# Gate and up products of 18 of 22 inner chunks as seven quarter products, in a float32 decoder trunk

## The chip, the core and the metric

The kernel runs on one core of a Trainium2 chip. The metric is the device time of one execution in microseconds (us). Engines: PE is TensorE, DVE VectorE, ACT ScalarE, POOL GpSimd, SP SyncE; each runs its own instructions in their order and waits on semaphores of the others. SP's and POOL's queues start transfers here.

## What is computed

A decoder trunk of two layers on 512 tokens of width 1024, all in float32. Six sub-layers, each with a norm before it and one behind it:

```python
def rms_norm(x, g):  return x * rsqrt(mean(x * x, -1) + 1e-6) * g
def swiglu(n, w_gate, w_up, w_down):          # 1024 -> 2816 -> 1024
    return (silu(n @ w_gate) * (n @ w_up)) @ w_down
...
f = swiglu(rms_norm(h, ffn_pre_g[layer, 0]), ...)
h = h + 0.5 * rms_norm(f, ffn_post_g[layer, 0])
h = h + rms_norm(mixer(rms_norm(h, mix_pre_g[layer])), mix_post_g[layer])
f = swiglu(rms_norm(h, ffn_pre_g[layer, 1]), ...)
h = h + 0.5 * rms_norm(f, ffn_post_g[layer, 1])
```

The mixer is a gated spatial unit (gMLP) in layer 0 and multi-head latent attention (MLA) in layer 1; between the layers keys and values are compressed once (`Shared`). The order is FFN 1, gMLP, FFN 2, Shared, FFN 3, MLA, FFN 4.

## The kernel before

Features lie on partitions, tokens along the free axis; the residual stream h is 8 chunks of 128 features by 512 tokens. TensorE multiplies float32r, so each operand is split exactly into a high and a low part, and each product is three matmuls: high by high, high by low, low by high (`mm3`, L391). The weight is the stationary operand (128x128), the activation the moving one (128 x 256 or 512).

Weights come in units of 512 KB (1024 inputs by 128 outputs, 128x1024 in memory), fetched by SP (`fetch`, L363) into one of WR = 3 raw buffers. `parts` (L369) splits a unit: a cast on ScalarE (tile `wh`), then a subtract on VectorE (`wl`), into one of WS = 6 split buffers. Activations live in SLOTS = 59 buffers of 128x512 (tiles `a`). PSUM banks are `mm`.

Nothing orders the program but a planner at build time, `Flow` (L111). The products are a list of items (L210), run in turn; what other engines do behind them are tasks, generators that yield what they wait for. With every instruction the planner books an estimated duration (`cost`, L77; recorded at L100, which is why nearly every row of the profile says L100) and issues tasks' steps and weight splits where the estimate says that their engine is free. The order on each engine is then fixed.

`ffn` (L651) has 22 inner chunks of 128. Chunks 0 and 1, and then 2, are done for the first half of the tokens (A, 256) and then for the second (B), since the halves of h come one after the other; from chunk 3 on all 512 tokens go at once. A chunk is 2 weights x 8 input chunks x 3 = 48 matmuls. The input is h times the gain, without R, the reciprocal root mean square along tokens: R is found later (`Norm.finish`, L482: squares are summed on POOL, a matmul takes the mean, POOL the root, a matmul `mm<-ident,r` spreads it, ScalarE copies it) and multiplied into the gate product in `glu` (L654), which then does Silu, the product with up, and the split of the result. The up product is not multiplied by R; the norm behind the sub-layer takes that into account (argument `norm` of `project`, L599).

The chunks come in groups (`FGROUPS`); behind each group `project` multiplies the group's chunks by w_down into 8 output chunks, which `Boundary` adds up and, behind the last group, norms and adds to h (L518, L551). `hook` puts the rotary tables into FFN 1, and `Shared` ran behind the first group of FFN 3.

Of the kernel before, what the change touches and what calls it, by code (L numbers as in the profile page):

```python
# [16 lines left out]
P = 128  # L17
# [16 lines left out]
FGROUPS = ((0, 8), (8, 15), (15, 22))  # L34
# [54 lines left out]

class Engine:  # L90
    """An engine, whose instructions are also put into the flow's estimate of time."""
# [19 lines left out]
class Flow:  # L111
    """The order of the program. Work that waits for other engines is a generator, which yields what it
    waits for: a condition (a callable), tensors (a list) or an engine that has less than so much to
    do (a pair). What engines do is followed by an estimate of each instruction's time."""
# [28 lines left out]
    def place(self, key, t, us):  # L143
        """Takes the first time from t on in which the engine has nothing to do."""
# [50 lines left out]
    def reach(self, t):  # L195
        """TensorE's next instruction can start at t: do what is due before."""
# [13 lines left out]
    def drive(self, items, fetch, parts):  # L210
        """Run the items. Units are fetched, and split into parts, before their time where there is room."""
# [14 lines left out]
    def get(self):  # L226
        if self.queue and len(self.raw) < WR:
            j, x = self.queue.pop(0)
            raw = self.fetch(*x)
            n = int(np.prod(x[1]))  # L230
# [3 lines left out]
            self.write(raw, self.dma + 2.0)  # L234
# [25 lines left out]
class Parts:  # L260
    """The two parts of each chunk of a tensor, and which halves of the tokens have been written."""
# [13 lines left out]
def decoder_kernel(ctx: ExitStack, tc: tile.TileContext, a: dict, out: bass.AP):  # L275
# [14 lines left out]
    # names given, units split  # L290
# [29 lines left out]
    # tables and clocks of the engines that the first products wait for  # L320
# [42 lines left out]
    def fetch(src, shape, spare=False):  # L363
        n = shape[0] * shape[1]
# [3 lines left out]

    def parts(raw, src, shape, spare=False):  # L369
        """The parts of each of a unit's chunks; `spare` units take room of activations."""  # L370
# [3 lines left out]
        count[1] += 1  # L374
        res = []
        for c0 in range(0, n, step):
# [10 lines left out]
            res += [(hi[:, x : x + m], lo[:, x : x + m]) for x in range(0, step, m)]  # L387
        return res

# [1 line left out]
    def mm3(ps, w, x, start, stop):  # L391
        """ps += w^T x from the parts of w (stationary) and x (moving)."""
# [30 lines left out]
    def rsqrt(x, n, out=None):  # L423
        """1 / sqrt of a few columns."""
# [14 lines left out]
    def token_mean(acc, lo, hi_, n):  # L439
        """Means of acc's columns over n features, by token on partitions."""  # L440
# [5 lines left out]
    def spread(c, n, diag):  # L446
        """Per-token scalars (token on partition, one column a tile) along the free axis, on all partitions."""
# [8 lines left out]
    class Squares:  # L456
        """Sums of chunks' squares."""
# [14 lines left out]
    class Norm:  # L472
        """Scalars of a pre-norm: R along tokens on all partitions, r by token, e = eps / r^2."""
# [32 lines left out]
    def gained(c, gains, outs, lo, hi_):  # L506
        """Split h[c] times each gain."""
# [10 lines left out]
    class Boundary:  # L518
        """Post-norm of a sub-layer's output, the residual sum, and what the next sub-layers read."""
# [31 lines left out]
        def finish(self, lo, hi_, norm):  # L551
            """For some tokens, whose f is f r where there is a norm before it."""
# [32 lines left out]
        def store(self, bc, lo, hi_):  # L585
            """The kernel's result; f has the gains already."""
# [12 lines left out]
    def project(source, ks, bnd, first, last, norm=None, width=NK):  # L599
        """source(d): the unit of output chunk d; ks(): its input."""  # L600
# [38 lines left out]
    def columns(us, x, rng, kouter):  # L639
        """Products of several column units with some tokens."""  # L640
# [10 lines left out]
    def ffn(i, prev, bnd, hook=None, shared=None):  # L651
        hid = {}

        def glu(f, rng, pg, pu):  # L654
            lo, hi_ = rng
            g = slot()[:, : hi_ - lo]
            norm = prev.norm
            yield norm.known(lo, hi_)
            V.tensor_tensor(g, pg, norm.R[:, lo:hi_], op=ALU.mult)
# [4 lines left out]
            SC.copy(hi[:, lo:hi_], g)  # L664
            V.tensor_tensor(lw[:, lo:hi_], g, hi[:, lo:hi_].bitcast(F32), op=ALU.subtract)
            hs.mark(c, lo, hi_)

# [3 lines left out]
        def run(us, fs, rng, kouter=False):  # L671
            banks = columns(us, prev.outs[0], rng, kouter)
            for j, f in enumerate(fs):
                flow.later(glu(f, rng, banks[2 * j], banks[2 * j + 1]))

        def add(gi, f0, f1):
# [12 lines left out]

            start = f0  # L690
            if gi == 0:
                start = f0 + 3
                kept = {}

                def keep(us, fs, rng, kouter):
                    kept[fs] = us
                    go(us, fs, rng, kouter)

# [7 lines left out]
                item(lambda us: keep(early["u"], q, A, False), (), 0)  # L706
                item(lambda us: go(kept[p], p, B, i > 0), (), 4)
                item(lambda us: go(kept[q], q, B), (), 0)
            for f in range(start, f1):
                item(lambda us, f=f: go(us, (f,), ALL), load(f))  # L710
            if gi == 0 and hook is not None:
                item(lambda us: hook())
            if gi == 0 and shared is not None:
                item(shared.run, shared.loads)
# [3 lines left out]
                lambda: prev.norm, f1 - f0,  # L718
# [154 lines left out]
    def rope_tables():  # L873
# [9 lines left out]
        def parts(x):  # L883
            """x as float32 parts of 12 bits, 12 bits and the rest."""
# [13 lines left out]
        # r less the nearest multiples of 2 pi 2^22, 2 pi 2^11 and 2 pi: exact but for what t collects,  # L898
        # which may take r a little out of range again
# [412 lines left out]
```

## Time and profile before

| | |
|---|---|
| time, median of 3 runs | 2021.34 us (2021.0 to 2021.54) |
| profiled execution, span from first to last instruction | 2020.5 us |
| instructions | 25023 |
| TensorE busy | 1976.6 us, 10064 matmuls |
| VectorE busy | 951.7 us, 1437 instructions |
| ScalarE busy | 717.7 us, 1176 instructions |
| GpSimd busy | 218.3 us, 358 instructions |
| mean granted TensorE clock | 0.993 |

Rows of groups give line, engine, operation, output<-inputs (numbers of tiles left out), shapes and count, then busy us and mean ns of one, and the idle time ahead. Rows of the timeline begin with start and duration in us. Rows of windows begin with the stretch and its length, then busy us of each engine (with instructions), and at the end granted clock, DMA share and GB/s. Rows of the DMA part end with KB each and the median us from issue to landing.

### The profile page before, as it was taken

The page shows a single profiled execution, that of the slowest core. Times are in us where ns is not written, and L with a number is a line of the kernel's source. Part 1 is how long each engine was busy: PE and PEld are TensorE (multiplying, and loading weights), DVE is VectorE, ACT ScalarE, POOL GpSimd, SP SyncE. Part 2 cuts the span into 40 slices and gives each one's busy share as a digit, 9 for nine tenths or more (in the row PEclk, how much of TensorE's full clock was granted, in tenths as well). Part 3 has the DMA queues.
Part 4 walks back from the last instruction along what each step waited for, and adds up shares of the span by engine and source line. Part 5 has one row for each costly group of instructions (what it writes and reads, how often), then busy time and mean ns, then how long its engine had stood idle before and what let it go on. Part 6 is the DMA issues. An engine that isn't in the chain of part 4 may idle for free.

```text
span 2020.5 us, 25023 instructions
## 1 busy us (share of the span) xinstructions
PE 1976.6 (98%) x10064; PEld 1685.8 (83%) x10064; DVE 951.7 (47%) x1437; ACT 717.7 (36%) x1176; POOL 218.3 (11%) x358
## 2 busy tenths in 40 slices
PE   8999999999999999999999999999999999999997
PEld 8888888888888888888888888888878898888886
DVE  6443344635635642333465443343767554234434
ACT  5232223433333432222243332223566553222222
POOL 4000000510001400000041010000521150000001
PEclk9999999999999999999999999999999999999999
DMA  6233333142333133333322233333121213332321
GB/s 205 84 99 94 99 96 113 53 136 73 96 103 108 40 115 94 93 96 104 104 74 84 76 114 97 99 93 97 43 73 63 81 46 105 94 100 88 105 84 43
DMA packets 56149, 184.94 MB, mean 92 GB/s; under 512 B 6176, under 2 KB 10400, under 8 KB 56032
## 3 DMA queue, kind: packets, MB, share of 16 engines
q1 hardware_dynamic: 54016, 179.85, 29.0%
q0 software_dynamic: 720, 2.36, 0.4%
q8 instruction: 79, 1.29, 0.3%
q10 hardware_dynamic: 1296, 1.12, 0.2%
q14 instruction: 38, 0.31, 0.0%
HBM read 181.21 MB, written 2.10 MB: 91 GB/s over the span
## 4 chain that ended last, share of the span: by engine, by line
PE 89%; DVE 5%; POOL 3%; ACT 2%; issue 1%; DMA 0%; SPq 0%; DVEq 0%; POOLq 0%; ACTq 0%
PE mm L100 89%; DVE a L100 3%; ACT a L100 1%; DVE h L100 1%; POOL nt L100 1%; POOL y L100 1%; DVE wl L100 1%; POOL a L100 1%; ACT wh L100 0%; POOL a L931 0%; DMA h<-in_xT 0%; DMA wr<-in_mla_w_o 0%; DVE m L100 0%; DVE x L100 0%; POOL r L100 0%
## 5 line engine op out<-in xcount | busy, mean ns | idle before, releaser
L100 PE MATMUL mm<-a,wh 128*128 128x512 f32 (+1 forms) x5584 | 1568.7, 367 | 3.4 <-ACT wh L100 1.3
L100 PEld LDWEIGHTS mm<-a,wh 128*128 128x128 f32 x5584 | 1009.8, 189 | 171.6 <-DVE a L100 1.8
L100 PE MATMUL mm<-a,wl 128*128 128x512 f32 (+1 forms) x2792 | 1020.7, 366 | 1.5 <-DVE wl L100 1.5
L100 ACT CAST wh<-wr 128x1024 fp32r<-128x1024 f32 (+2 forms) x340 | 344.5, 1017 | 999.3 <-PE mm L100 713.2
L100 PEld LDWEIGHTS mm<-a,wl 128*128 128x128 f32 x2792 | 528.5, 189 | 86.0 <-DVE wl L100 2.0
L100 DVE TENSOR_TENSOR a<-mm,a 128x512 f32<-128x512 f32 (+3 forms) x380 | 228.6, 609 | 709.7 <-PE mm L100 698.9
L100 DVE TENSOR_TENSOR wl<-wr,wh 128x1024 fp32r<-128x1024 f32 (+2 forms) x340 | 403.4, 1190 | 216.4 <-ACT wh L100 204.2
L100 POOL TENSOR_TENSOR a<-a,a 128x256 f32<-128x256 f32 x162 | 139.6, 869 | 1165.7 <-ACT a L100 1162.3
L100 PE MATMUL mm<-a,a 128*128 128x256 f32 (+3 forms) x896 | 131.6, 299 | 2.3 <-ACT a L100 2.3
L100 ACT ACTIVATE a<-a 128x256 f32<-128x256 f32 (+1 forms) x216 | 105.5, 504 | 69.4 <-DVE a L100 68.9
L100 PEld LDWEIGHTS mm<-a,a 128*128 128x128 f32 x896 | 119.8, 191 | 7.5 <-ACT a L100 3.2
L100 DVE TENSOR_TENSOR a<-a,a 128x512 fp32r<-128x512 f32 (+4 forms) x171 | 107.9, 633 | 28.1 <-ACT a L100 21.2
L100 ACT CAST a<-a 128x512 fp32r<-128x512 f32 (+2 forms) x134 | 77.8, 583 | 75.6 <-DVE a L100 74.7
L100 PE MATMUL mm<-wh,a 128*128 128x512 f32 x288 | 93.0, 398 | 0.0
L100 POOL TENSOR_TENSOR y<-x,minus_half 128x2 f32<-128x2 f32 (+1 forms) x28 | 22.1, 788 | 527.7 <-DVE x L100 527.6
L100 ACT ACTIVATE a<-h,vec 128x256 fp32r<-128x256 f32 (+1 forms) x104 | 52.1, 520 | 52.6 <-DVE h L100 50.1
L100 PEld LDWEIGHTS mm<-wh,a 128*128 128x128 f32 x288 | 55.1, 191 | 11.7 <-issue 0.2
L100 DVE SCALAR_TENSOR_TENSOR a<-h,vec,a 128x256 fp32r<-128x256 f32 (+1 forms) x104 | 58.1, 578 | 6.0 <-ACT a L100 5.9
L100 PE MATMUL mm<-wl,a 128*128 128x512 f32 x144 | 56.8, 395 | 0.0
L100 DVE SCALAR_TENSOR_TENSOR h<-a,vec,h 128x256 f32<-128x256 f32 x80 | 48.2, 623 | 0.0
L100 ACT COPY a<-mm 128x512 f32<-128x512 f32 (+1 forms) x66 | 33.3, 512 | 32.7 <-PE mm L100 32.7
L100 DVE TENSOR_TENSOR a<-a,mm 128x256 f32<-128x256 f32 x94 | 36.2, 412 | 15.7 <-PE mm L100 13.4
(83 smaller groups left out, 453.0 us busy)
## 6 DMA issues: line engine op xcount, KB each, us to landing
wr<-in_ffn_w_up SPq DMA_DIRECT2D x88, 512.0 KB, 3.5
wr<-in_ffn_w_gate SPq DMA_DIRECT2D x87, 512.0 KB, 3.6
wr<-in_ffn_w_down SPq DMA_DIRECT2D x64, 448.0 KB, 3.3
wr<-in_ffn_w_down SPq DMA_DIRECT2D x32, 512.0 KB, 3.5
wr<-in_w_in_u SPq DMA_DIRECT2D x16, 512.0 KB, 3.7
wr<-in_w_in_v SPq DMA_DIRECT2D x16, 512.0 KB, 3.6
wr<-in_gmlp_w_out SPq DMA_DIRECT2D x16, 512.0 KB, 3.5
wr<-in_mla_w_o SPq DMA_DIRECT2D x8, 512.0 KB, 3.5
```

The lines of the kernel that those rows point to most:

```text
L100: res = fn(*args, **kwargs)
```

## The change

Chunks 0 to 3 of each FFN stay as they were (`PLAIN = 4`), but for one multiply: the up product is now multiplied by R too. Chunks 4 to 21 form 9 pairs. A pair's product is a 2x2 block product for each of gate and up: the outputs' two chunks by the inputs' two halves (a11, a12, a21, a22 hold 4 input chunks of gate and of up each, 512 KB), times the input's two halves by the tokens' two halves (b11 to b22). Seven products of quarter size replace the eight, in Winograd's form of Strassen's scheme, each with sums of weights or of inputs:

| product | weights | input | accumulates in bank |
|---|---|---|---|
| a11 | a11 (raw buffer x) | b11 | X |
| s2 | x = x + s1 | t2 = b22 - b12 + b11, up to the order of the sums | Y |
| s1 | s1 = a21 + a22 | e1 = b11 - b12 | V |
| a12 | a12 (raw buffer y) | b21 | X, on top |
| s3 | a11 + a21 | n3 = b12 - b22 | Y, on top |
| a22 | a22 | t4 = t2 - b21 | Z |
| s4 | y = y + x | b22 | V, on top |

Each is 2 x 4 x 3 = 24 matmuls of N = 256. Signs are arranged so that only sums of weights occur. s1 and the weights of s3 are made by a load through SP and an accumulating DMA through POOL into the same buffer; x = x + s1 and y = y + x by VectorE.

The seven forms of the input need h times gain times R. `prepare` makes them for each FFN once R of both halves is known: for each of 4 chunks 2 multiplies of 512 columns, 4 sums of 256 and 7 splits of 256. A product is put into the order only once all are there in the planner's book. Behind products, tasks combine the banks (`of_a11` to `of_s4`): p1 copied from X by ScalarE, u2 = p1 - Y, u3 = Y - p1, x = u3 - V (after which V may be accumulated into again), and so on; `out` applies Silu and the product and splits.

Further: groups are 0-8, 8-16, 16-22; WR = 5, WS = 5, SLOTS = 61; the planner's cost of a matmul has another formula; Shared stands behind the last pair of FFN 3, ahead of the last output products; the hook of FFN 1 stands ahead of the pairs.

```diff
-FGROUPS = ((0, 8), (8, 15), (15, 22))
+FGROUPS = ((0, 8), (8, 16), (16, 22))
+PLAIN = 4
+NP = (NF - PLAIN) // 2
+H = S // 2
-WR, WS, SLOTS = 3, 6, 59
+WR, WS, SLOTS = 5, 5, 61
...
-        return max(n * (1 if aps[1].dtype in (F32R, BF16) else 4) / 2370.0, 0.03)
+        return max((n + 31) * (1 if aps[1].dtype in (F32R, BF16) else 4) / 2400.0, 0.03)
...
+            def summed(base, more):
+                t = load_raw(src[base], NK * P)
+                nc.gpsimd.dma_start(t, src[more], accum_op=ALU.add)
+                return t
...
+        def before(self):
+            raw = self.pair.raw
+            if self.name == "s2":
+                V.tensor_tensor(raw["x"], raw["x"], raw["s1"], op=ALU.add)
+
+        def behind(self):
+            raw = self.pair.raw
+            if self.name == "a12":
+                V.tensor_tensor(raw["y"], raw["y"], raw["x"], op=ALU.add)
...
-            V.tensor_tensor(g, pu, g, op=ALU.mult)
+            V.tensor_tensor(u, pu, R, op=ALU.mult)
+            V.tensor_tensor(g, u, g, op=ALU.mult)
...
+        def part(name, src):
+            t = slot(F32R)
+            SC.copy(t[:, :H], src)
+            V.tensor_tensor(t[:, H:], src, t[:, :H].bitcast(F32), op=ALU.subtract)
+            forms.setdefault(name, []).append((t[:, :H], t[:, H:]))
+
+        def prepare():
+            norm = prev.norm
+            yield norm.known(0, S)
+            name, base = prev.gains[0]
+            half = NK // 2
+            for c in range(half):
+                n1, n2, e, t = slot(), slot(), slot(), slot()
+                for n, k in ((n1, c), (n2, c + half)):
+                    V.scalar_tensor_tensor(
+                        n, h[k], col(name, base + k), norm.R, op0=ALU.mult, op1=ALU.mult
+                    )
+                b11, b12, b21, b22 = n1[:, :H], n1[:, H:], n2[:, :H], n2[:, H:]
+                part("b11", b11)
+                V.tensor_tensor(e[:, :H], b11, b12, op=ALU.subtract)
+                V.tensor_tensor(t[:, :H], b22, e[:, :H], op=ALU.add)
+                yield ("V", T_LEAD)
+                part("t2", t[:, :H])
+                part("e1", e[:, :H])
+                part("b21", b21)
+                yield ("V", T_LEAD)
+                V.tensor_tensor(e[:, H:], b12, b22, op=ALU.subtract)
+                part("n3", e[:, H:])
+                V.tensor_tensor(t[:, H:], t[:, :H], b21, op=ALU.subtract)
+                part("t4", t[:, H:])
+                part("b22", b22)
+                yield ("V", T_LEAD)
...
+            ORDER = (("a11", "X", "b11"), ("s2", "Y", "t2"), ("s1", "V", "e1"), ("a12", "X", "b21"),
+                     ("s3", "Y", "n3"), ("a22", "Z", "t4"), ("s4", "V", "b22"))
...
+                for w in range(2):
+                    o = ps[:, w * H : (w + 1) * H]
+                    for k in range(half):
+                        hi, lw = us[0][w * half + k]
+                        th, tl = forms[x][k]
+                        flow.reach(max(flow.when(y) for y in (hi, lw, th, tl)))
+                        at = first and w == k == 0
+                        PE.matmul(o, hi, th, start=at, stop=False, skip_group_check=True)
+                        PE.matmul(o, hi, tl, start=False, stop=False, skip_group_check=True)
+                        end = k == half - 1
+                        PE.matmul(o, lw, th, start=False, stop=end, skip_group_check=True)
...
+            def of_s3(self):
+                u3 = self.t["u3"] = slot()
+                x = slot()
+                yield [self.banks["Y"]]
+                V.tensor_tensor(u3, self.banks["Y"], self.t["p1"], op=ALU.subtract)
+                V.tensor_tensor(x, u3, self.banks["V"], op=ALU.subtract)
+                self.read.add("V")
+                self.out(x, self.f + 1, H)
```

What stands on the engines, first on TensorE in the second FFN, behind chunks 0 to 2 (before: chunk 3 begins; `a` is the input's high and low part):

```order
L100 MATMUL mm_5745<-a_5077,wh_5569 128x512 [waits DVE_49]
L100 MATMUL mm_5745<-a_5078,wh_5569 128x512
L100 MATMUL mm_5745<-a_5077,wl_5570 128x512
L100 MATMUL mm_5745<-a_5079,wh_5569 128x512
L100 MATMUL mm_5745<-a_5080,wh_5569 128x512
```

After the change the same chunk 3 ends with the first row here (bank mm_6889), and then the first pair's products stand in pieces of 3: mm_7039 is a11's bank, mm_7071 s2's, mm_7106 s1's, and a_7014 is the fourth b11. Left out behind the fourth row are pieces of the same kind, 27 matmuls of N = 256 in all ahead of the last two rows.

```order
L104 MATMUL mm_6889<-a_6193,wl_6812 128x512
L104 MATMUL mm_7039<-a_6723,wh_6882 128x256 [waits DVE_49,Activation_49]
L104 MATMUL mm_7039<-a_6723,wh_6882 128x256
L104 MATMUL mm_7039<-a_6723,wl_6883 128x256
...
L104 MATMUL mm_7106<-a_6969,wh_7065 128x256 [waits DVE_49]
L104 MATMUL mm_7106<-a_6969,wl_7066 128x256
L104 MATMUL mm_7039<-a_7014,wh_6882 128x256 [waits Activation_49]
L104 MATMUL mm_7039<-a_7014,wh_6882 128x256 [waits DVE_49]
```

So chunk 4's 48 wide matmuls have given way to pieces that wait for the forms as they come. On VectorE at the same place, before, the products of chunk 3 (bank mm_5745, mm_5746) are combined with one weight split (`wl`) between each two steps:

```order
L100 TENSOR_TENSOR a_5806<-mm_5745,a_5093 128x512 [waits PE_49,Pool_49]
L100 TENSOR_TENSOR wl_5808<-wr_5676,wh_5807 128x1024 [waits DMAHW2_49,Activation_49]
L100 TENSOR_TENSOR a_5806<-mm_5746,a_5806 128x512 [waits PE_49,Activation_49]
L100 TENSOR_TENSOR wl_5812<-wr_5730,wh_5811 128x1024 [waits DMAHW3_49,Activation_49]
L100 TENSOR_TENSOR a_5237<-a_5806,a_5236 128x512 [waits Activation_49,Pool_49]
```

After (a_6195 is R, mm_6888 and mm_6889 chunk 3's products, wr_6357 the buffer x, a_7014 the fourth b11):

```order
L104 TENSOR_TENSOR a_6995<-mm_6888,a_6195 128x512
L104 TENSOR_TENSOR a_6996<-mm_6889,a_6195 128x512 [waits PE_49]
L104 TENSOR_TENSOR wr_6357<-wr_6357,wr_6161 128x1024 [waits DVE_49]
L104 TENSOR_TENSOR a_6995<-a_6996,a_6995 128x512 [waits DVE_49,Activation_49]
L104 TENSOR_TENSOR wl_7130<-wr_6815,wh_7129 128x1024 [waits DMASW4_49]
L104 TENSOR_TENSOR a_6331<-a_6995,a_6330 128x512 [waits Activation_49]
L104 SCALAR_TENSOR_TENSOR a_7008<-h,vec,a_6195 128x512
L104 SCALAR_TENSOR_TENSOR a_7009<-h,vec,a_6195 128x512
L104 TENSOR_TENSOR a_7014<-a_7008,a_7014 128x256 [waits Activation_49]
```

The fourth chunk of the forms is begun behind chunk 3's evacuation and behind weight splits and sums of the first pair. Last, VectorE between two pairs in the second FFN, where before stood the rows of the kind shown above. mm_7858 is the bank Y of the pair that ends, mm_7892 its V, a_7851 its p1; wr_7744 and wr_7777 are the next pair's x and s1:

```order
L104 TENSOR_TENSOR wr_7744<-wr_7744,wr_7777 128x1024 [waits DMASW1_49,DVE_49]
L104 TENSOR_TENSOR wl_7951<-wr_7744,wh_7950 128x1024 [waits PE_49,Activation_49]
L104 TENSOR_TENSOR a_7948<-a_7948 128x256 [waits Activation_49]
L104 TENSOR_TENSOR wl_7986<-wr_7777,wh_7985 128x1024 [waits PE_49,Activation_49]
L104 TENSOR_TENSOR a_7811<-a_7948,a_7810 128x256 [waits Activation_49]
L104 TENSOR_TENSOR a_7983<-mm_7858,a_7851 128x512
L104 TENSOR_TENSOR a_7984<-a_7983,mm_7892 128x512 [waits DVE_49]
```

The last two rows are u3 and x = u3 - V; the next pair's sum x + s1, which waits for an accumulating DMA, and the splits of s2 and s1 now stand ahead of them.

More of the change, by code (lines that the diff above doesn't have):

```diff
@@ L374, in parts @@
         count[1] += 1
+        form = src if isinstance(src, Form) else None
+        if form:
+            form.before()
         res = []
@@ L387, in parts @@
             res += [(hi[:, x : x + m], lo[:, x : x + m]) for x in range(0, step, m)]
+        if form:
+            form.behind()
         return res
@@ L662, in glu, with keep_hidden @@
+            V.tensor_tensor(g, u, g, op=ALU.mult)
+            keep_hidden(f, lo, hi_, g)
+        def keep_hidden(f, lo, hi_, x):
             hs, c = hid[f]
             hi, lw = hs.pairs[c]
-            SC.copy(hi[:, lo:hi_], g)
-            V.tensor_tensor(lw[:, lo:hi_], g, hi[:, lo:hi_].bitcast(F32), op=ALU.subtract)
+            SC.copy(hi[:, lo:hi_], x)
+            V.tensor_tensor(lw[:, lo:hi_], x, hi[:, lo:hi_].bitcast(F32), op=ALU.subtract)
             hs.mark(c, lo, hi_)
+        forms = {}
@@ L688, in go, with product @@
                 run(us, fs, rng, kouter)
+            def product(us, pair, step):
+                begin()
+                pair.product(us, *step)
             start = f0
             if gi == 0:
-                start = f0 + 3
+                start = PLAIN
                 kept = {}
@@ L697, in keep @@
                     go(us, fs, rng, kouter)
+                    flow.later(prepare())
                 p, q = (f0, f0 + 1), (f0 + 2,)
@@ L705, in add @@
                     item(lambda us: early.update(u=us), load(q[0], True), 0)
-                item(lambda us: keep(early["u"], q, A, False), (), 0)
+                item(lambda us: go(early["u"], q, A, False), (), 0)
                 item(lambda us: go(kept[p], p, B, i > 0), (), 4)
-                item(lambda us: go(kept[q], q, B), (), 0)
-            for f in range(start, f1):
-                item(lambda us, f=f: go(us, (f,), ALL), load(f))
+                item(lambda us: go(early["u"], q, B), (), 0)
+                for f in range(f0 + 3, PLAIN):
+                    item(lambda us, f=f: go(us, (f,), ALL), load(f))
             if gi == 0 and hook is not None:
                 item(lambda us: hook())
-            if gi == 0 and shared is not None:
-                item(shared.run, shared.loads)
+            for f in range(start, f1, 2):
+                pair = Pair(f)
+                for step in Pair.ORDER:
+                    item(
+                        lambda us, pair=pair, step=step: product(us, pair, step),
+                        [(Form(pair, step[0]), (NK, P), False)],
+                    )
+            if gi == len(FGROUPS) - 1:
+                item(lambda us: forms.clear())
+                if shared is not None:
+                    item(shared.run, shared.loads)
             project(
@@ L717, in add @@
                 lambda: group["x"], bnd, gi == 0, gi == len(FGROUPS) - 1,
[L718 removed]
+                lambda: None, f1 - f0,
             )
```

98 lines of the change are left out of this document (92 added, 6 removed).

## The prediction

> **What bounds the kernel now.** I read the page first: the busy line, then the chain that ended last.
>
> ```profile
> span 2020.5 us, 25023 instructions
> PE 1976.6 (98%) x10064; PEld 1685.8 (83%) x10064; DVE 951.7 (47%) x1437; ACT 717.7 (36%) x1176; POOL 218.3 (11%) x358
> PE 89%; DVE 5%; POOL 3%; ACT 2%; issue 1%; DMA 0%; SPq 0%; DVEq 0%; POOLq 0%; ACTq 0%
> ```
>
> TensorE is busy 98% of the span, so only fewer or shorter matmuls can save much; VectorE, at 47%, has room on the average, but not at every place. The windows view with TensorE alone, over the second FFN (its 512-token chunks and output products) and over a stretch behind a wait, and the timeline at the end of two FFNs' two-half parts, give the price of a matmul:
>
> ```profile
> 714.00:1020.00 306.00, 306.00 (x1352) 1.00 0.33 100
> 386.20:392.80 6.60, 4.79 (x13) 0.50 0.29 79
> ...
> 388.01 1.23 PE L100 MATMUL mm<-half,y 128*128 128x128 f32 x4 [3.95 <-POOL y L100]
> ...
> 1081.11 5.92 PE L100 MATMUL mm<-a,a 128*128 128x256 f32 x48
> 1086.87 0.63 PE L100 MATMUL mm<-a,wh 128*128 128x512 f32 x2
> ```
>
> 306 us for 1352 matmuls of N=512 is 226.3 ns each, without idle time. 48 matmuls of N=256 start at 1081.11 and the next one at 1086.87: 5.76 us, 120 ns each. Half the width costs 53% of the time. And after an idle time of 3.95 us the granted clock is 0.50 for some 6.6 us.
>
> **The products: gain.** In each FFN 18 chunks of 48 N=512 matmuls (864 x 226.3 ns = 195.5 us) become 9 pairs of 7 x 24 N=256 matmuls (1512 x 120 ns = 181.4 us): 14.1 us less. The seven-for-eight saving of 12.5% shrinks to 7%. Over four FFNs: **-56**. A pair of chunks goes from 21.7 to 20.16 us.
>
> The Trainium skill ("TensorE: Matmul & The Clock Gate", Back-to-back issue gap) gives the warm spacing of isolated matmuls as N/2.4 + 2.5 ns, so 109.2 and 215.8 ns, and says itself that this is too little at small N. By it the gain would be 864 x 215.8 - 1512 x 109.2 = 21.3 us an FFN, 85 in all; the 48-matmul rows say otherwise (120 ns).
>
> **The forms: the largest loss.** The pairs read normed input in seven forms, which can be begun only when the scalars R of both token halves are there, and every product needs all four chunks of its form. R of the second half is copied late in the two-half part; the N=512 stream begins 9 to 14 us behind it:
>
> ```profile
> 35.25 0.37 ACT L100 COPY a<-mm 128x256 f32<-128x256 f32 x1
> 49.01 0.63 PE L100 MATMUL mm<-a,wh 128*128 128x512 f32 x2
> 704.46 0.37 ACT L100 COPY a<-mm 128x256 f32<-128x256 f32 x1 [4.43 <-PE mm L100]
> 713.61 0.63 PE L100 MATMUL mm<-a,wh 128*128 128x512 f32 x2
> 1077.72 0.37 ACT L100 COPY a<-mm 128x256 f32<-128x256 f32 x1 [4.43 <-PE mm L100]
> 1667.35 0.37 ACT L100 COPY a<-mm 128x256 f32<-128x256 f32 x1 [4.63 <-PE mm L100]
> 1677.58 0.63 PE L100 MATMUL mm<-a,wh 128*128 128x512 f32 x2
> ```
>
> Behind that stream's start TensorE has chunk 3 (48 x 226.3 ns = 10.9 us) and then, by the order, 27 matmuls on the first three chunks of the forms (3.2 us; 51 in the first FFN, 6.1 us) before the first one that reads the fourth. So it runs dry at 66.0, 727.7, 1101.0 and 1691.7 us. VectorE's side, from rows that follow each other without a gap:
>
> ```profile
> 20.77 0.68 DVE L100 TENSOR_TENSOR a<-wr,a 128x512 fp32r<-128x512 f32 x1
> 21.38 0.47 DVE L100 SCALAR_TENSOR_TENSOR a<-h,vec,a 128x256 fp32r<-128x256 f32 x1
> ...
> 708.22 2.36 DVE L100 TENSOR_TENSOR wl<-wr,wh 128x1024 fp32r<-128x1024 f32 x2
> 710.49 0.75 DVE L100 TENSOR_TENSOR a<-mm,a 128x256 f32<-128x256 f32 x2
> 711.16 1.22 DVE L100 TENSOR_TENSOR wl<-wr,wh 128x1024 fp32r<-128x1024 f32 x1
> 712.29 0.76 DVE L100 TENSOR_TENSOR a<-a,a 128x256 fp32r<-128x256 f32 x2
> 712.96 0.42 DVE L100 TENSOR_TENSOR a<-mm,a 128x256 f32<-128x256 f32 x1
> ...
> L100 DVE SCALAR_TENSOR_TENSOR a<-h,vec,a 128x512 fp32r<-128x512 f32 x8 | 5.5, 744 | 0.0
> ```
>
> From start to start a 1024-wide split takes 1.14 us, a 512-wide step 0.61, a 256-wide one 0.335; a 512-wide scalar-tensor step 0.744 by its group, less the 0.08 by which such rows overlap, 0.66. By the order VectorE has, from the first normed chunk to the subtract that ends the fourth b11: 8 x 0.66 + 46 x 0.335 + 8 x 1.14 + 4 x 0.61 = 32.2 us; the 8 of 1024 are the pairs' own weight splits and sums, which stand between the forms. It starts at R's copy plus 0.37: ready at 737.0, 1110.3 and 1699.9 us. In the first FFN the fourth b11 is there after 25.2 us of such rows, but between it and the subtract that ends the fourth t2, the next that TensorE needs, lie 15.8 us more by the same steps, mostly the rotary tables' 512-wide rows: 35.6 + 41 = 76.6. The stalls are 10.6, 9.3, 9.3 and 8.2 us: **+37**. At the end of each stands one uncovered cast on ScalarE, a subtract and two handovers (0.37 + 0.42 and some 0.1 each): **+4**. The bounds: VectorE may also stand and wait for a bank in between (+2 each), or part of the 512-wide rows falls ahead of R's second half for another reason (-2 each).
>
> Such stalls are broken up only by pieces of 3 matmuls, so the clock row above applies: of the 6.6 us at clock 0.50 above, 4.79 were busy, 2.4 us lost; four times is 10. If the bits of work between keep the clock, nothing is lost. I take **+8**, 0 to 14.
>
> The Trainium skill ("TensorE: Matmul & The Clock Gate", HAM oscillation) says that TensorE's idle gaps must stay under some 3.4 us, or it falls to half clock; this speaks against a change that opens gaps of 8 to 10 us. The trace agrees: 3.95 us was enough.
>
> **Weights.** A pair moves seven units of 512 KB, not four, two of them by accumulating DMA. Rows of the DMA part and of the groups:
>
> ```profile
> q1 hardware_dynamic: 54016, 179.85, 29.0%
> wr<-in_ffn_w_up SPq DMA_DIRECT2D x88, 512.0 KB, 3.5
> a<-in_w_sT POOLq DMA_DIRECT2D x4, 256.0 KB, 5.3
> L732 POOL DMA_DIRECT2D a<-in_w_sT x4 | 2.3, 568 | 0.0
> ```
>
> 29% of 2020.5 us for 179.85 MB is 1.7 us for 512 KB: seven are 12 of a pair's 20 us, or 15 if an add costs two. The capacity is there. No row shows an accumulating DMA; plain rows bound its landing: 3.5 us if like SP's 512 KB, 10.6 if like two of POOL's 256 KB, one behind the other. I take POOL's 5.3 and half of 1.7 for the other 256 KB: 6.2. What it may take: by the order the buffer for the next pair's x comes free with y = y + x, right behind V's read of the pair before, some 1.2 us into a pair; x and the sum's base load follow (3.5 + 1.7 = 5.2 us): 6.4. On VectorE x = x + s1 and the split of s2 stand ahead of s1's split, which can begin at s3's end and a cast of 1.05 (120 matmuls, 14.4 us, so 15.4): x = x + s1 is due at 15.4 - 2 x 1.14 = 13.2. That leaves 6.8 us, so **0**, by little; each us beyond is paid at 24 of the pair changes (6 in each FFN; the others stand behind output products).
>
> POOL issues these DMAs among the sums of squares of the boundary before each of FFNs 2 to 4: two issues of 0.57 us, in front of steps that TensorE waits for, 6 x 0.57 = **+3** (0 if beside a wait; 6 if an issue also waits for its base load).
>
> **The evacuation of a pair.** In a pair s4 accumulates into the bank V of s1, which must first be read by x = u3 - V, behind s3. After s3's end TensorE has a22 (24) and 10 matmuls of the next a11: 34 x 0.12 = 4.08 us. Behind s3's end by the order: the next s1's cast, since it takes the split buffer that s3 frees, its subtract, one small subtract, u3, x.
>
> ```profile
> L100 ACT CAST wh<-wr 128x1024 fp32r<-128x1024 f32 x264 | 277.2, 1052 | 752.3 <-PE mm L100 474.2 <-issue 260.9 <-DMA wr<-in_gmlp_w_out 6.5
> L100 DVE TENSOR_TENSOR a<-mm,a 128x512 f32<-128x512 f32 x234 | 161.6, 691 | 635.0 <-PE mm L100 634.3 <-ACT a L100 0.7
> ```
>
> 1.05 + 1.14 + 0.34 + 0.61 + 0.69 = 3.83, and four handovers of 0.1: some 4.2 to 4.4 us against 4.08, 0.1 to 0.3 us late in each of 36 pairs: **+10** at the upper end, which I take since ScalarE's and VectorE's other rows can only delay it; bounds 0 and 36 (1 us each). VectorE itself holds: 9 x 1.14 + 5 x 0.61 + 8 x 0.335 = 16.0 of 20.2 us a pair.
>
> **Nothing.** The extra multiply in the plain chunks (0.61 us) lies under a chunk's 10.9 us; Shared's move and the regrouped output products (same count) put the same work elsewhere. What they would cost uncovered is under 3 us.
>
> **The sum.** 2020.5 - 56 + 37 + 4 + 8 + 3 + 10 = 2026.5 us of span, with one profiled execution's rows. The median of the runs shown, 2021.3, lies 0.8 above that span: **2027 us**. With every loss at its lower or upper bound (29 to 45, 4, 0 to 14, 0 to 6, 0 to 36) it would be 1998 or 2070; I take 2005 to 2047 as its own range, since the ends will not all be met at once. What this kernel's measurement can tell from no change is some 0.2%, 4 us.
>
> **The rivals.**
>
> *The cover holds* (faster). The stalls come, but no clock is lost, POOL waits anyway, and s4 is never late: 2020.5 - 56 + 37 + 4 + 0.8 = 2006; where half of the weight splits among the forms were done before R, 4 x 4 x 1.14 = 18 us of the stalls would go too: 1988. For it: ScalarE and VectorE have idle time in every pair. Against it: the order, which puts these splits between the forms, and the 3.95 us row. 0.19.
>
> *The accumulating DMA lands late* (slower). If it takes 8.5 to 10.6 us, x = x + s1 waits, and with it on VectorE the splits of s2 and s1, then u3 and x: 1.7 to 3.8 us at 24 places, 41 to 91 us: 2068 to 2118. It decides from 6.8 us on. For it: the 5.3 us of POOL's transfers of half the size. Against: one large transfer need not take as long as two. 0.15.
>
> *The evacuation is later* (slower). One copy of ScalarE (0.58) and one 512-wide row (0.69) more stand ahead of V's read: 1.27 x 36 = 46 in place of 10: 2063. For it: ScalarE's copies and Silu of the same pair are due there. Against: the planner's order shows few of them between. 0.09.
>
> *Half the width in half the time* (faster). At 226.3 / 2 = 113 ns a matmul of N=256 the products would save 98 in place of 56: 1985. Against it stand the 48-matmul rows (120 ns). 0.01. The spacing that the page of the Trainium skill gives, above, comes near this case.
>
> **How the numbers follow.** Forecast 0.56: of it 0.12 below the 0.2% bound, 0.16 within, 0.28 above. With the rivals: faster 0.12 + 0.19 + 0.01 = 0.32, same 0.16, slower 0.28 + 0.15 + 0.09 = 0.52. Cases of both signs hold much; the likeliest alone spans 2005 to 2047. The range goes from 1988 to 2066: it leaves out the lowest 0.02 of the cover's case, the half-time case (0.01), nearly all of the late DMA's (0.15) and 0.02 of the evacuation's, and holds 0.8.
>
> **What would show it.** Right: in each FFN one or two idle times of TensorE of together 8 to 11 us behind chunk 3, released by VectorE, granted clock near 0.5 behind them; 24 matmuls of N=256 in 2.88 us within pairs; waits of some tenths at s4's first matmul. Wrong: no idle time behind chunk 3 (VectorE's steps are shorter, or its weight splits ran before); VectorE waiting for the accumulating DMA in front of x = x + s1; idle TensorE in front of s4 by more than 1 us a pair; or N=256 blocks not at 120 ns when weights change at each matmul pair.

## The result, and the profile after

| | time, us | against before |
|---|---|---|
| before | 2021.38, median of 4 (2021.0 to 2021.54) | |
| changed | 2043.69, median of 4 (2041.86 to 2045.97) | 1.0111 [1.0096, 1.0125] |

Slower by 1.1%. The forecast was 2027 us with its own range from 2005 to 2047, so this is its upper end. The page of the changed kernel, its span, busy times, chain and two DMA queues:

```profile
span 2044.3 us, 31598 instructions
PE 1945.3 (95%) x12608; PEld 1778.1 (87%) x12608; DVE 1321.7 (65%) x2105; ACT 922.6 (45%) x1612; POOL 281.0 (14%) x430
q1 hardware_dynamic: 59200, 198.73, 29.8%
q0 software_dynamic: 11088, 40.11, 11.3%
PE 71%; DVE 13%; DMA 5%; ACT 4%; POOL 3%; issue 3%; SPq 0%; POOLq 0%; DVEq 0%; ACTq 0%
```

TensorE is busy 31 us less, but it no longer carries 89% of the chain that ended last (it has 71%): VectorE rose from 5% to 13%, and DMAs, which had none, have 5%. Where the 24 us of span came in shows when the span is cut at the same events in both kernels: where chunk 3 of an FFN begins, and the spread of the last post-norm's scalar at its end. The windows view with TensorE alone, of the kernel before; rows are the first FFN, the gMLP with its boundaries, the second FFN, the third, the attention with its boundaries, and the fourth:

```profile
49.00:388.00 339.00, 334.81 (x1562) 1.00 0.31 94
388.00:713.60 325.60, 321.17 (x1724) 0.99 0.29 91
713.60:1049.50 335.90, 333.26 (x1568) 1.00 0.32 99
...
1086.90:1444.80 357.90, 354.95 (x1659) 1.00 0.30 93
1444.80:1677.60 232.80, 222.75 (x1420) 0.99 0.21 63
1677.60:2010.40 332.80, 329.16 (x1538) 1.00 0.29 88
```

The same stages of the changed kernel:

```profile
49.40:387.60 338.20, 325.82 (x2204) 0.98 0.50 140
387.60:718.60 331.00, 320.76 (x1720) 0.99 0.28 90
718.60:1058.30 339.70, 325.87 (x2212) 0.98 0.51 140
...
1096.30:1457.40 361.10, 346.22 (x2292) 0.98 0.47 130
1457.40:1702.00 244.60, 227.84 (x1424) 0.97 0.21 63
1702.00:2034.20 332.20, 319.55 (x2174) 0.98 0.46 127
```

The four FFNs together are only 5.6 us longer (-0.8, +3.8, +3.2, -0.6). The other 18 us lie where no matmul was changed: 5.4 in the gMLP's stage and 11.8 in the attention's, and some tenths at the start and in the short boundary left out. (The cut at the first FFN's end is good to some 0.6 us, since the spread comes in two pieces there.) In the attention's stage part of it is clock: the mean granted clock falls from 0.99 to 0.97, some 16 us at half clock against 3.

Inside an FFN, the second one. TensorE's timeline behind chunk 3, and the windows there:

```profile
732.65 0.28 PE L104 MATMUL mm<-a,wl 128*128 128x256 f32 x1
739.90 1.09 PE L104 MATMUL mm<-a,wh 128*128 128x256 f32 x2 [6.97 <-ACT a L104]
...
740.00:746.00 6.00, 6.00 (x27) 0.50 0.69 143
746.00:752.00 6.00, 6.00 (x52) 1.00 0.61 184
```

The last of the 27 matmuls on three chunks of the forms, then 7 us of nothing, then half clock: 27 matmuls in 6 us, where the next 6 us hold 52. VectorE, at its first normed chunk and then in that time:

```profile
707.79 1.42 DVE L104 SCALAR_TENSOR_TENSOR a<-h,vec,a 128x512 f32<-128x512 f32 x2 [2.61 <-ACT a L104]
...
735.12 1.23 DVE L104 TENSOR_TENSOR wr<-wr,wr 128x1024 f32<-128x1024 f32 x1
736.25 0.70 DVE L104 TENSOR_TENSOR a<-a,a 128x512 f32<-128x512 f32 x1
736.86 1.23 DVE L104 TENSOR_TENSOR wl<-wr,wh 128x1024 fp32r<-128x1024 f32 x1
737.99 0.70 DVE L104 TENSOR_TENSOR a<-a,a 128x512 fp32r<-128x512 f32 x1
738.59 1.42 DVE L104 SCALAR_TENSOR_TENSOR a<-h,vec,a 128x512 f32<-128x512 f32 x2
739.92 0.43 DVE L104 TENSOR_TENSOR a<-a,a 128x256 fp32r<-128x256 f32 x1
```

No idle time: a weight sum, a weight split and chunk 3's evacuation, and only then the fourth chunk of the forms. Between pairs, the same FFN, TensorE at a first matmul of s4, and VectorE ahead of it:

```profile
864.69 0.50 PE L104 MATMUL mm<-a,wh 128*128 128x256 f32 x2 [2.04 <-DVE a L104]
...
857.89 1.23 DVE L104 TENSOR_TENSOR wr<-wr,wr 128x1024 f32<-128x1024 f32 x1 [2.81 <-DMA wr<-in_ffn_pairs]
860.28 1.23 DVE L104 TENSOR_TENSOR wl<-wr,wh 128x1024 fp32r<-128x1024 f32 x1 [1.17 <-ACT wh L104]
861.42 0.42 DVE L104 TENSOR_TENSOR a<-a 128x256 f32<-128x256 f32 x1
861.76 1.22 DVE L104 TENSOR_TENSOR wl<-wr,wh 128x1024 fp32r<-128x1024 f32 x1
862.90 0.42 DVE L104 TENSOR_TENSOR a<-a,a 128x256 fp32r<-128x256 f32 x1
863.23 0.68 DVE L104 TENSOR_TENSOR a<-mm,a 128x512 f32<-128x512 f32 x1
863.95 0.69 DVE L104 TENSOR_TENSOR a<-a,mm 128x512 f32<-128x512 f32 x1
```

Read from below: TensorE waits for x = u3 - V (863.95), which stands behind u3, the splits of s1 and s2, and x = x + s1, which waited 2.81 us for the accumulating DMA. Over the whole run, from the waits view and the DMA part:

```profile
DVE wr L104 <- DMA wr<-in_ffn_pairs: 19.0, 12, 2.8
...
wr<-in_ffn_pairs SPq DMA_DIRECT2D x180, 512.0 KB, 3.4
wr<-in_ffn_pairs POOLq DMA_DIRECT2D x72, 512.0 KB, 6.0
```

Twelve of the 36 sums x + s1 waited, 19 us together.

### The profile page after: what moved, and what is told of

Same layout as the page of the kernel before. It is cut to its first block, busy times and chain, and to the rows that moved or that the text cites. A ratio compares the mean times of both kernels' runs of the same rounds, so it can differ in the third digit from the quotient of the medians.

```text
span 2044.3 us, 31598 instructions
## 1 busy us (share of the span) xinstructions
PE 1945.3 (95%) x12608; PEld 1778.1 (87%) x12608; DVE 1321.7 (65%) x2105; ACT 922.6 (45%) x1612; POOL 281.0 (14%) x430
## 3 DMA queue, kind: packets, MB, share of 16 engines
q1 hardware_dynamic: 59200, 198.73, 29.8%
q0 software_dynamic: 11088, 40.11, 11.3%
## 4 chain that ended last, share of the span: by engine, by line
PE 71%; DVE 13%; DMA 5%; ACT 4%; POOL 3%; issue 3%; SPq 0%; POOLq 0%; DVEq 0%; ACTq 0%
PE mm L104 71%; DVE a L104 8%; DMA wr<-in_ffn_pairs 4%; DVE wl L104 2%; ACT a L104 2%; POOL a L104 2%; ACT wh L104 2%; DVE h L104 1%; DVE wr L104 1%; POOL y L104 1%; POOL nt L104 1%; DMA h<-in_xT 0%; DVE x L104 0%; POOL a L1133 0%; DVE m L104 0%
## 5 line engine op out<-in xcount | busy, mean ns | idle before, releaser
L104 PE MATMUL mm<-a,wh 128*128 128x256 f32 (+1 forms) x7280 | 1606.0, 317 | 39.9 <-ACT a L104 26.3
L104 PEld LDWEIGHTS mm<-a,wh 128*128 128x128 f32 x7280 | 1216.8, 193 | 126.7 <-ACT a L104 27.5
L104 PE MATMUL mm<-a,wl 128*128 128x256 f32 (+1 forms) x3640 | 1145.7, 315 | 4.7 <-DVE wl L104 4.7
L104 DVE TENSOR_TENSOR wl<-wr,wh 128x1024 fp32r<-128x1024 f32 (+2 forms) x448 | 537.5, 1202 | 328.3 <-ACT wh L104 324.1
L104 ACT CAST wh<-wr 128x1024 fp32r<-128x1024 f32 (+2 forms) x448 | 456.2, 1022 | 646.5 <-PE mm L104 459.4
L104 PEld LDWEIGHTS mm<-a,wl 128*128 128x128 f32 x3640 | 703.4, 193 | 44.7 <-DVE wl L104 5.4
L104 DVE TENSOR_TENSOR a<-mm,a 128x512 f32<-128x512 f32 (+4 forms) x272 | 151.6, 576 | 185.3 <-PE mm L104 178.6
L104 DVE TENSOR_TENSOR a<-a,a 128x256 fp32r<-128x256 f32 (+4 forms) x431 | 189.7, 469 | 41.3 <-ACT a L104 33.9
L104 ACT CAST a<-a 128x256 fp32r<-128x256 f32 (+1 forms) x318 | 127.1, 430 | 163.0 <-DVE a L104 162.6
L104 DVE TENSOR_TENSOR a<-a,mm 128x512 f32<-128x512 f32 (+1 forms) x238 | 132.8, 577 | 26.2 <-PE mm L104 23.1
```

The costliest lines, as they stand in the source:

```text
L104: res = fn(*args, **kwargs)
```

## The experiments

Theories. A: waiting for the forms, with the half clock behind it, is the largest loss (some 38 us). A': accumulating DMAs that land late delay s4 at pair changes. For the 18 us outside the FFNs there are three candidates: Shared's move, the buffers (five split units in place of six), and the new price of a matmul, which is the duration that the planner books for one. Each run is set against executions of the kernel before taken beside it. e1 and e2 leave out work that the result needs, so they tell only times.

| run | us, median | against before |
|---|---|---|
| e1, changed, forms without work | 2001.28 | 0.9904 [0.9889, 0.9919] |
| e2, changed, without accumulating DMAs | 2026.18 | 1.0027 [1.0016, 1.0038] |
| e3, changed, six plain chunks | 2009.10 | 0.9938 [0.9918, 0.9958] |
| e4, before, Shared late | 2020.47 | 0.9997 [0.9987, 1.0006] |
| e5, before, buffers 5, 5, 61 | 2024.45 | 1.0019 [1.0010, 1.0029] |
| e6, before, new price | 2035.10 | 1.0070 [1.0055, 1.0085] |
| e7, changed, s1 loaded early | 2033.30 | 1.0061 [1.0046, 1.0076] |
| e8, six plain chunks and s1 early | 1996.76 | 0.9876 [0.9858, 0.9894] |
| e9, as e8 with the old price | 1983.77 | 0.9813 [0.9799, 0.9828] |
| e10, changed, old price | 2046.00 | 1.0122 [1.0105, 1.0139] |
| e11, as e9 with buffers 4, 6, 59 | 1982.53 | 0.9807 [0.9792, 0.9821] |
| e12, before, new price and buffers | 2039.53 | 1.0092 [1.0075, 1.0109] |

**e1: the forms without their work.**

```diff
...
-                for n, k in ((n1, c), (n2, c + half)):
-                    V.scalar_tensor_tensor(
...
+                for x, p in (("b11", lo1), ("t2", hi1), ("e1", lo1), ("b21", lo2),
+                             ("n3", hi2), ("t4", lo2), ("b22", hi2)):
+                    forms.setdefault(x, []).append(p)
```

> The changed kernel without the work of the forms: all seven forms are taken from halves of the parts of h times gain that are there anyway, so the sums, the 28 splits of 256 columns and the factor R are left out. Theory A (waiting for the forms is the largest loss: 30.7 us of idle TensorE behind chunk 3 in the four FFNs, and 7.4 us of half clock behind it): 2044 - 38 = about 2006 us, no idle time over 1 us behind chunk 3. Rival (VectorE and ScalarE are behind in the pairs anyway, and the time comes back there): 2030 us or more.

42.4 us less than the changed kernel, 4 more than expected. (The timeline has 29.1 us of idle TensorE behind chunk 3, not the 30.7 named there.) The second FFN's stage, and TensorE behind its chunk 3, in the windows view of e1:

```profile
707.60:1033.30 325.70, 321.55 (x2213) 1.00 0.54 147
...
735.00:745.00 10.00, 10.00 (x84) 1.00 0.51 148
```

The stage takes 325.7 us, 10.2 less than before the change: with the forms for nothing most of the products' gain reaches the end, and full clock stays. A holds, and the rival does not: the time didn't come back in the pairs.

**e2: no accumulating DMAs.** The second addend of s1 and of s3 is left out, the order is otherwise that of the changed kernel.

```diff
-                nc.gpsimd.dma_start(t, src[more], accum_op=ALU.add)
```

> The changed kernel without the 72 accumulating DMAs (the second addend of s1 and s3 is left out; order and all else as in the changed kernel). Theory A' (they land late at some pair changes, which shows as TensorE's idle times of 0.5 to 2 us ahead of s4, some 14 us and 2 us of half clock, and stand in the boundaries among the squares on GpSimd, some 10 us): 2018 to 2030 us. Rival (the waits ahead of s4 come from the evacuation by itself, the boundaries from VectorE's added rows): 2040 to 2044 us.

17.5 us less than the changed kernel, as A' had it. The second FFN and the attention's stage of e2:

```profile
715.80:1050.70 334.90, 324.72 (x2211) 0.98 0.37 117
1446.80:1687.30 240.50, 225.49 (x1423) 0.98 0.19 60
```

4.8 us came in this FFN and 4.1 in the attention's stage, where two of these DMAs are issued by GpSimd between sums of squares. The gMLP's stage, with two as well, did not get shorter.

**e7: the same loads in another order.** All the work is done, and the order of loads differs: s1 takes the buffer that s1 of the pair before left early. With the order go two numbers by which the planner books these loads.

```diff
-            self.moved = dict(s2=3, s1=0, s3=3, s4=0).get(name, 1)
-            self.late = 5.0 if name in ("s2", "s3") else 2.0
+            self.moved = dict(a11=4, s2=0, s1=0, s3=3, s4=0).get(name, 1)
+            self.late = 5.0 if name == "s3" else 2.0
...
             if self.name == "a11":
+                raw["s1"] = summed(a21, a22)
+                flow.write(raw["s1"], flow.dma + 5.0)
                 raw["x"] = load_raw(src[a11], NK * P)
                 return raw["x"]
             if self.name == "s2":
-                raw["s1"] = summed(a21, a22)
-                flow.write(raw["s1"], flow.dma + 5.0)
                 return raw["x"]
```

> The changed kernel with the loads of a pair in another order: s1's base load and accumulating DMA are issued ahead of x's load, so that they take the buffer that s1 left early in the pair before and not the one that y = y + x frees late. Theory A' (s4 is late because x = x + s1 waits for the accumulating DMA): VectorE's 19 us of waits in front of x = x + s1 and TensorE's in front of s4 go: 2026 to 2032 us. Rival (s4 is late because of what VectorE and ScalarE have to do, so the wait moves): 2038 to 2044 us.

10.4 us less than the changed kernel, 1 us short of the expected range: the waits for the DMA in front of x = x + s1 are no longer among the waits. The second FFN's row in e7:

```profile
717.30:1051.70 334.40, 323.55 (x2210) 0.98 0.52 144
```

It is as short as without the DMAs (334.9): in this FFN the wait was all of their cost. So it is in the other three (335.6, 358.7 and 328.9 us, in e2 335.6, 358.7 and 328.3). What e2 saved beyond e7, 7 us, lies outside the FFNs, some 3 of it in the attention's stage; the DMAs' issue on GpSimd and their traffic are left for it, and no run tells these apart.

**e3 and e8: more cover for the forms, then with s1 early.**

```diff
-PLAIN = 4
+PLAIN = 6
```

> The changed kernel with PLAIN = 6: chunks 4 and 5 stay plain too, eight pairs remain. Theory A: two chunks more (21.8 us of TensorE, against some 9.4 us more of VectorE) cover the forms: 38 us of idle and half-clocked time go, 4 x 1.6 us of the products' gain and one pair's waits with them: about 2012 us. Rival (the time of the forms is lost wherever they are made): 2044 to 2050 us.

> Both corrections: PLAIN = 6 and s1 loaded ahead of x. Theory A with A' (the two losses are independent): 2009 - 8/9 of what the early load brings by itself (12 to 17 us) = 1994 to 1999 us. Rival (the six plain chunks already gave the DMAs their time): 2005 to 2009 us.

e3 takes 2009.1 us, 34.6 less than the changed kernel: two plain chunks cost some 6 us of the gain and take the whole stall. This also beats the kernel before. e8 takes off 12.3 us more, and e7 alone took 10.4, so the two losses add, as far as e3's spread (2002.7 to 2013.4) can tell.

**e4, e5, e6, e12: what was lost where nothing was multiplied differently.** Each is the kernel before with one or two lines of the change: the first of these for e4, the second for e5, the third for e6, the last two for e12.

```diff
-            if gi == 0 and shared is not None:
+            if gi == len(FGROUPS) - 1 and shared is not None:
...
-WR, WS, SLOTS = 3, 6, 59
+WR, WS, SLOTS = 5, 5, 61
...
-        return max(n * (1 if aps[1].dtype in (F32R, BF16) else 4) / 2370.0, 0.03)
+        return max((n + 31) * (1 if aps[1].dtype in (F32R, BF16) else 4) / 2400.0, 0.03)
```

> The kernel before, with one part of the change alone: Shared stands ahead of the last output products of the third FFN. Theory A'' (its move crowds the boundary into the attention, where the changed kernel lost 12 us outside the FFNs): 2026 to 2033 us. Rival (that loss belongs to the pairs and their DMAs): 2021 us.

> The kernel before, with the buffers of the changed one alone: WR, WS, SLOTS = 5, 5, 61. Outside the FFNs the changed kernel lost 18 us (6 ahead of the second FFN, 12 ahead of the fourth), and neither the forms nor the accumulating DMAs nor Shared's move explain them. Theory B (five split buffers in place of six leave TensorE less to do while norms are finished): 2030 to 2042 us. Rival: 2021 us.

> The kernel before, with the planner's new price of a matmul alone. Theory C (the price, 4.6% more for N = 512 and 10.7% more for N = 256, shifts weight splits and norm steps in the boundaries and costs those 18 us): 2030 to 2042 us. Rival (the price hardly moves anything that is waited for): 2019 to 2023 us.

> The kernel before, with the planner's new price and the buffers 5, 5, 61 together, and no pairs. If these two parts of the change make up what it lost outside the FFNs (6 us ahead of the second FFN, 12 ahead of the fourth): 2021 + 3 + 14 = about 2038 us, with the stage from the first FFN's end to the second's chunk 3 longer by some 6 us, and the attention's by 6 to 12. If they overlap: 2033 to 2036 us; if not at all the cause: 2025 us or less.

Shared's move cost nothing: that theory fell. The buffers cost 3.4 us, less than their theory had and more than the rival, and the price 14.0, as its theory had it; together 18.5. The gMLP's and the attention's stage in e12:

```profile
386.10:718.50 332.40, 322.62 (x1730) 0.99 0.28 87
1453.30:1694.00 240.70, 226.00 (x1423) 0.98 0.20 61
```

6.8 and 7.9 us longer than before the change, 14.7 of the 17.3 by which the span grew. In the changed kernel it was 5.4 and 11.8; the attention's 11.8 are these 7.9 and the 4.1 that went with the accumulating DMAs (e2). The price acts in both stages (2.4 and 5.7 us in e6), the buffers in the gMLP's alone (3.9 in e5). Both show in the same wait. TensorE's idle time ahead of results of GpSimd, in the waits view of the kernel before and of the changed one:

```profile
PE mm L100 <- POOL a L100: 5.3, 7, 1.7
...
PE mm L104 <- POOL a L104: 18.3, 14, 3.6
```

With the rows for y and r it is 22.3 us in all before, 24.0 in e5, 32.5 in e6, 37.5 in e12 and 38.5 in the changed kernel; without the accumulating DMAs (e2) it is still 37.5. One place is the boundary ahead of the second FFN: TensorE's waits there in e12, in the changed kernel, and in the kernel before:

```profile
675.62 0.61 PE L100 MATMUL mm<-mean,a 128*128 128x1 f32 x4 [1.85 <-POOL a L100]
679.61 0.80 PE L100 MATMUL mm<-ident,y 128*128 128x128 f32 x2 [2.00 <-POOL y L100]
```

```profile
675.61 0.61 PE L104 MATMUL mm<-mean,a 128*128 128x1 f32 x4 [1.85 <-POOL a L104]
679.61 0.79 PE L104 MATMUL mm<-ident,y 128*128 128x128 f32 x2 [2.01 <-POOL y L104]
```

```profile
681.61 0.60 PE L100 MATMUL mm<-ident,y 128*128 128x128 f32 x3 [2.07 <-POOL y L100]
```

The first of these two waits was not there before. From the second on the granted clock is 0.5 for some 5 us in both runs, where before the change it stayed at 1.00 behind the one. The price changes none of the work. It changes when the planner lets the tasks behind a product go, and so, it seems, what TensorE has left to do while GpSimd finishes a sum; which of the shifted steps matters was not tried.

**e10, e9, e11: the old price in the changed kernel, alone and with both corrections, and then six split buffers.**

> The changed kernel with the planner's old price alone. Theory C: 2044 - 14 = 2030 us, gained in the boundaries and in the attention. Rival: 2040 us or more.

> PLAIN = 6, s1 loaded ahead of x, and the planner's old price of a matmul. Theory C (the price costs the changed kernel what it costs the kernel before, 14 us, and independently of the rest): about 1983 us. Rival (pairs of N = 256 need the new price, or the loss overlaps with the others): 1994 to 2005 us.

> As the kernel with all three corrections, with WR, WS, SLOTS = 4, 6, 59. If six split units are worth in the changed kernel what five cost the kernel before (3 us) and nothing waits for the missing raw buffer: 3 us less than that kernel, about 1980 us. Rival (four raw buffers make a pair's seven loads late): 10 us or more above it.

In the changed kernel the old price alone gained nothing: that expectation failed. The first FFN's stage and the attention's in e10, and TensorE behind chunk 3 of its first FFN:

```profile
48.60:390.00 341.40, 324.83 (x2197) 0.98 0.50 138
1460.00:1699.00 239.00, 226.94 (x1419) 0.97 0.21 65
...
73.01 0.58 PE L104 MATMUL mm<-a,wh 128*128 128x256 f32 x1 [10.14 <-ACT a L104]
```

The attention got 5.6 us back, but the first FFN is 3.2 us longer, with an idle time of 10.1 us and one of 2.1 in place of three of 8.8 together, and the fourth is 3.6 us longer: the new price put the uncovered forms in a somewhat better order. With six plain chunks the forms are covered, and the old price is worth 13.0 us (e8 to e9). The page of e9:

```profile
span 1980.7 us, 30875 instructions
PE 1933.6 (98%) x12320; PEld 1757.4 (89%) x12320; DVE 1293.0 (65%) x2065; ACT 905.0 (46%) x1576; POOL 270.2 (14%) x422
PE 90%; DVE 3%; POOL 3%; ACT 2%; issue 1%; DMA 0%; SPq 0%; DVEq 0%; POOLq 0%; ACTq 0%
```

TensorE carries 90% of the chain again, and the kernel is 1.9% faster than before the change. e11 is 1.2 us below it, which this measurement does not tell from nothing: neither the 3 us expected of six split buffers nor the loss of 10 us that the rival feared. It beats both kernels as e9 does.

## Why the prediction was right, and where it was not

The forecast was 2027 us with slower as the likeliest side; it came out at 2044. By its steps:

- **Products, -56.** Right. Matmuls of both widths, counted in each stage at 120 and 226.7 ns, come to 57 us less in the four FFNs. The isolated spacing (109 ns) and the rival of half the time in half the width fall with it.
- **Forms, +37 and +4.** The mechanism was right and the place too: in the first FFN TensorE ran dry at 65.8 us and had its last idle time there end at 76.6, forecast 66.0 and 76.6. The idle times behind chunk 3 are 8.8, 7.0, 6.9 and 6.4 us, 29 in all, against 10.6, 9.3, 9.3 and 8.2. In the second FFN VectorE's steps, forecast at 32.2 us, took 32.5, from 707.79 to the end of the subtract's step at 740.25. What moved is their surroundings, since the boundary ahead had become longer: R's copy came 2.9 us later than assumed (707.3) and TensorE ran dry 5.2 us later (732.9), so the stall is smaller. The +4 was not there: the waiting matmul (739.90) needs only ScalarE's cast, which was done before VectorE began the subtract (739.92). e1 puts forms, handovers and clock together at 42, the forecast at 49; e3 takes them away. Idle and half-clocked time behind chunk 3 add up to 36.5 of these 42; where e1's other 6 us lie is open.
- **Clock, +8.** Right: matmuls at half clock behind these four stalls lost 7.4 us, added up over those that took about twice their time. The Trainium skill's rule ("TensorE: Matmul & The Clock Gate", HAM oscillation: no idle gap over some 3.4 us) agrees with all four, whose longest idle times are 4.3, 7.0, 6.9 and 6.4 us. But 2.04 us at s4 was also followed by half clock, a loss of 1.6 us, while 2.07 us in the kernel before (at 681.6) was not, so 3.4 us is no safe limit here.
- **Accumulating DMAs, 0 and +3.** This step failed. "That leaves 6.8 us, so 0, by little": the landing taken was 6.2 us, and the median of all 72 is 6.0, but that mixes two kinds. Those for s1, which this wait is about, landed after 7.1 us in the median (5.1 to 9.1), 23 of 36 after more than 6.8; those for s3 after 5.4. Twelve were late, three in each FFN, half of the 24 changes named, with landings of 7.4 to 9.1 us, and TensorE's idle times ahead of s4 there add up to 10 us. They cost 10 us as a wait (e7) and 17.5 in all (e2). A rival had the mechanism, at 41 us and more, since it took all 24 changes to be late. Why the first kind lands later than the second was not tried.
- **Evacuation, +10.** Too high: where no DMA was late, s4's product took 2.98 us in place of 2.88, 0.1 us in each of 36 pairs, so 4 us, the lower end of the 0.1 to 0.3 worked out. The waits of 0.2 to 2 us belong to the step above.
- **What had no term.** The list of things that cost nothing named the extra multiply, Shared's move and the regrouping; of these only Shared's move was tried, and it is right (e4). The planner's price and the buffers were not in it at all. They lie behind no instruction that the prediction looked at, and cost 18.5 us in the kernel before (e12). The order that the build made shows how far such numbers reach: s4 stands behind 10 matmuls of the next pair, which no item of the kernel says.

With the measured sizes the sum is 2020.5 - 57 + 29 + 7 + 17.5 + 4 + 18.5 = 2039.5, and 0.8 outside the span: 2040 of 2044 us. The rest is not taken apart; part of it is an idle time of 3.6 us at the third FFN's end, which the runs with pairs and the new price show, and which is 1.9 us with the old one (e9, e10). The terms do not simply add, though: the price taken back alone gained nothing (e10), since what it brought in the attention went again in two FFNs whose forms are uncovered. What remains open is which of the steps that the price moved makes GpSimd's sums late.

So the side was forecast partly by luck. The forecast had slower by 6 us, from forms, clock, DMA issues and evacuation against the products. At their measured sizes its own terms come to nothing, -57 + 29 + 7 + 17.5 + 4 = +0.5 us, and that only with 17.5 for the DMAs, which it had put at 3. By this sum the 1.1% is the price and the buffers, for which it had no term, though e10 warns against taking such a sum to the last us. What the forecast had right is the mechanism of the forms and the sizes of products and clock.

## What to carry to other kernels

Work that becomes due all at once behind a barrier (here seven forms behind the last norm scalar) needs cover, which is counted in the bottleneck engine's time and by the order in its queue: two more plain chunks gave up 6 us of the gain and still brought 35. A number that only an estimate uses is an edit like any other: compare what stands in the queues everywhere, not only where the code changed. And a transfer whose time spreads is judged by its longest, and by its own kind and not by the median of all, against the slack of the wait that stands ahead of others in its queue; giving it a buffer that comes free earlier was a matter of a few lines.

## What the runs showed of the hardware

An accumulating DMA of 512 KB into memory on the chip landed after 6.0 us in the median (5.1 to 9.1), a plain one of the same weights after 3.4. In time on the DMA engines it is dearer by nearly two: 37.75 MB took 11.3% of 2044.3 us less the 0.4% of 2020.5 us that this queue had before, 3.1 us for each 512 KB, against 1.6 us for a plain one (198.73 MB in 29.8%). The Trainium skill ("Collectives: The Full Stack", The bandwidth ceiling: the fold count and why AG ≠ RS ≠ AR) explains why a ReduceScatter has half the rate of an AllGather by the two source reads of its adds, with a measured ratio of 1.93. The ratio here is 1.9, for one core's own transfers; that it has the same reason no run here shows.
